# Order of epilogues, bank copies and weight preparation at the passage between two kinds of seven-product quads

## The chip, the cores and the metric

The kernel runs on one core of a Trainium2 chip. The core has a tensor engine (PE, with its own queue for weight loads), a vector engine (DVE), a scalar engine (ACT), GpSimd (POOL), and a sync engine (SP) that issues most transfers. Each engine works through its own instructions in order and waits on semaphores of the others. The metric is the device time of one launch in microseconds. Times are the median of three runs.

## The reference

Two blocks work on 512 tokens of 1024 features. The first block normalises and modulates its input (shift, scale and gate come from a small matrix product with a condition vector), runs a gated delta rule and a retention over chunks, projects, and ends with a gated feed-forward network. The second block has two layers, each of a feed-forward network, a mixer and another feed-forward network. So there are five feed-forward networks, all of this form:

```
def swiglu(h, w_in, w_out):
    gate, up = jnp.split(h @ w_in, 2, axis=-1)
    return (jax.nn.silu(gate) * up) @ w_out
x = x + g2 * swiglu(modulate(rms_norm(x, norm_ffn_g[layer]), sh2, sc2), w_ffn_in[layer], w_ffn_out[layer])
x = layer_norm(ALPHA * x + 0.5 * swiglu_2(x, ffn_w1[l, 0], ffn_w2[l, 0]), ln_g[l, 0], ln_b[l, 0])
```

All operands are float32. The hidden width of each network is 2816.

## The kernel before

**Precision.** A float32 matrix is held as two rounded parts, hi and lo. ACT casts hi, DVE subtracts to get lo (lines 79 to 81 for data, `cast` and `rest` at lines 163 to 166 for weights). A product is three matmuls: hi by hi, hi by lo, lo by hi.

**Seven products.** A product of 2 by 2 blocks is done with seven block products in place of eight (class `Quad`). Sums of weight blocks are made on DVE (`sum`, line 161). Sums of data blocks are made once, by `Left.sums` (lines 113 to 120), and split by `Left.puts`. The result blocks share partial results. A partial result is copied from one PSUM bank to another by ACT so that two products can go on from it: line 177 after product 1, lines 179, 180 and 181 after products 3, 4 and 5. The three banks that take copies are `sd0`, `sd1` and `sd2`. The other results lie in `pj` tiles.

**A feed-forward network** (`ffn`, line 285). Two units of hidden columns are done plainly with eight products, then the rest with quads, in four groups. Of a group, *gated quads* come first: they multiply the activations `XA` by the gate and up weights. When a result block is finished its *epilogue* runs: `c11` is a silu, `c12` (lines 257, 259) adds and multiplies and so gives half of a hidden tile `h`, `c12b` (line 260) splits that half into `hl`, `c22` subtracts, `c21` (lines 264, 265) gives the other half of `h`, `c21b` makes the sums of `h` and splits the second half, and `c21c` splits the sums. For the last gated quad of a group (`last`) all of `c21` is one step, `at_once`. Then come two *output quads* which multiply `hl` by the second weight matrix and add into `X`. They need the hidden tiles of all gated quads of the group. The first three groups end this way, the fourth in plain products. So each network has three places where the last gated quad of a group gives way to its output quads. They are called *passages* here: first, second and third passage of a network, fifteen in all. At the first and second passage an output quad has 3 hidden tiles (18 matmuls of 256 columns in a block product), at the third 2 (12 matmuls).

**What sets the order.** `run_quads` (line 190) writes the order of PE, ACT, DVE and SP out by hand. It goes step by step through the list of block products. At a step it issues the matmuls of product s, the epilogue and bank copy of product s-1 (`after`), the sums of weights, and the cast and lo part of the weights of product s+2. Normally the epilogue stands first and the weights after it. At a passage, after products 6 and 7 of the last gated quad, the flag `late` (line 224) puts weights first. At a passage the first products of both output quads follow each other, and only then come their other products (lines 197 to 201).

**The start of a network** (lines 308 to 317). While the plain units run, the sums of `XA` are made, part 1 of all four pairs of tiles and then part 0. They are called through `e.sums`. In the first network the modulated activations are not kept in `X`, so `sums` at line 1256 first adds hi and lo again (`again`, line 1253), two additions of 128x512 for a part of a pair.

**The condition product** (`ada_piece`, line 1261). Half rows of its weights are multiplied by the condition and added up over eight pieces. A ninth step sums over partitions by four matmuls. Parts 0 to 2 are done on ACT (scale, line 1276) and POOL (addition, line 1277), later parts on DVE (lines 1278, 1279). Parts 6 and 7 are issued in `first_b` during the projection that ends the first block's mixer.

Of the kernel before, what the change touches and what calls it, by code (L numbers as in the profile page):

```python
# [14 lines left out]
H0=slice(0,256); H1=slice(256,512); FULL=slice(0,512)  # L15
# [174 lines left out]
def run_quads(e, quads, extra):  # L190

    ET=mybir.EngineType
    seq=[]; left=None; done=set()
    for i,q in enumerate(quads):
        if q.needs and left: seq.append((left,7)); left=None
        if q not in done: seq.append((q,1))
        if q.needs: seq.append((quads[i+1],1)); done.add(quads[i+1])
        if left: seq.append((left,7))  # L200
        seq+=[(q,j) for j in (2,3,4,5,6)]; left=q
    seq.append((left,7))
    pos={(id(q),j):s for s,(q,j) in enumerate(seq)}
    at={}; free=-99
    for q in quads:
        g=lambda j: pos[id(q),j]
        for s,t in ((g(1)-6,0),(g(3)-9,5),(g(2)-8,6),(max(g(3)-6,free),3),(g(3)-4,1),(g(3)-3,2),(g(5),4)): at.setdefault(s,[]).append((q,t))
        free=g(5)-1
    with e.tc.manual_schedule(engines={ET.PE,ET.Activation,ET.DVE,ET.SP}):
        for s in range(min(at),len(seq)+1):  # L210
            for q,t in at.get(s,[]):
                if t in (0,5,6): q.load(e,t)
            put=None; keep=None
            if s>0: put=seq[s-1]
            if 0<=s<len(seq):
                q,j=seq[s]
                for d in q.needs:
                    if j==1: d.all(6)
                    if j==3: d.all(7)
                if j==2 and put==(q,1): q.after(e,1); put=None  # L220
                q.mm(e,j)
                if j==7 and s+1<len(seq) and seq[s+1][1]==2: keep=seq[s+1][0]
            nx=seq[s+2] if 0<=s+2<len(seq) else None
            late=put and put[1] in (6,7) and any(put[0] is q.needs[-1] for q in quads if q.needs)
            def weights():
                for q,t in at.get(s,[]):
                    if t in (1,2,3,4): q.sum(e,t)
                if nx and late: nx[0].cast(e,nx[1]); nx[0].rest(e,nx[1])
            if late: weights()
            if put and not (put[1]==1 and put[0] in done): put[0].after(e,put[1])  # L230
            if not late: weights()
            for q in quads:
                for j in (2,5,6,7):
                    if s>0 and (q,j)!=put: q.step(j)
            if keep in done: keep.after(e,1)
            for f in extra.get(s,[]): f()
            if nx and not late: nx[0].cast(e,nx[1]); nx[0].rest(e,nx[1])
        for q in quads:
            for j in (2,5,6,7): q.all(j)
# [11 lines left out]
def gated(e, H, i, hscale, sums, last):  # L251
# [11 lines left out]
    def c21(ps):  # L263
        g=tmp(e); nc.scalar.activation(g,ps,AF.Silu)
        nc.vector.scalar_tensor_tensor(u.h[:,2:4,:],pair(g),hscale,pair(u.t),op0=ALU.mult,op1=ALU.mult)
    v=nc.vector
    def part(p): u.s=H.sums(e,i,u.h[:,0:2,:],u.h[:,2:4,:],p,v,p and u.s); return u.s
    def c21b(ps):
        if sums: u.p0=part(0); u.p1=part(1)
        if last: H.puts(e,i,0,u.p0)  # L270
        H.second(e,i,u.h[:,2:4,:])
        if last: H.puts(e,i,1,u.p1)
    def c21c(ps):
        if sums and not last: H.puts(e,i,0,u.p0); H.puts(e,i,1,u.p1)
    u.c11,u.c12,u.c22,u.c21=[c11],[c12,c12b],[c22],[c21,c21b,c21c]
    if last:
        def at_once(ps): c21(ps); c21b(ps)
        u.c21=[at_once]
    return u

GAB=4
# [3 lines left out]
def ffn(e, w1, w2, acc, hscale, ln):  # L285

    nc=e.nc
    with ExitStack() as cf:
# [3 lines left out]
        H=Left(t,2,3); HP=Left(t,3,3)  # L292
# [17 lines left out]
                unit(j,sl)  # L310
                if j%2: into_left(e,H,j//2,hs[j//2],0 if sl is H0 else 1,False)
        for q in range(PLAIN-1): hsums(q)
        for p in (1,0):
            for i in range(4): e.sums(p,i)
        for j in range(halves,2*PLAIN):
            unit(j,FULL)
            for half in (0,1): into_left(e,H,j//2,hs[j//2],half,False)
# [1 line left out]
        for g,(j0,n) in enumerate(GROUPS):  # L319
            last=g==len(GROUPS)-1  # L320
# [86 lines left out]
class LN(Norm):  # L407
# [18 lines left out]
    def finish(s,sl):  # L426
        e=s.e; nc=e.nc; X=e.X; h=s.half[sl.start]
        ps=psum(e,"ps")
# [11 lines left out]
        for i in range(4):  # L440
# [4 lines left out]
                m=2*i+j; nc.scalar.activation(X[:,m,sl],d[:,j,:],AF.Identity,scale=s.g[:,m:m+1],bias=s.b[:,m:m+1])  # L445
                if s.out is not None: s.out(m,sl)
            if s.out is None: s.to_left(sl,i,X[:,2*i:2*i+2,sl])
        if sl is H1: e.sums=lambda part,i: e.XA.puts(e,i,part,e.XA.sums(e,i,X[:,2*i:2*i+2,H0],X[:,2*i:2*i+2,H1],part))

def proj_units(units, first):  # L450

# [781 lines left out]
class RMS(Norm):  # L1233
# [4 lines left out]
    def finish(s,sl):  # L1238
        e=s.e; nc=e.nc; X=e.X; h=s.half[sl.start]
        ps=psum(e,"ps"); tokstat2(e,ps,0,pair(h.Q),e.ones1024[:,0:1])  # L1240
# [12 lines left out]
        def again(i,o):  # L1253
            t=pair(tmp(e)); A=e.XA.t
            nc.vector.tensor_add(t,A[:,o:o+2,i,0,:].bitcast(F32),A[:,o:o+2,i,1,:].bitcast(F32)); return t
        def sums(part,i):
            a,b=[X[:,2*i:2*i+2,h] for h in (H0,H1)] if s.b is None else (again(i,0),again(i,2))
            e.XA.puts(e,i,part,e.XA.sums(e,i,a,b,part))
        if sl is H1: e.sums=sums

def ada_piece(e,D,at,part,k,tag,raw):

# [9 lines left out]
    raw=raw()  # L1272
    nc.sync.dma_start(raw,D["ada2"][16+part*4+k//2][:,(k%2)*512:(k%2)*512+512])
    c=e.cc[:,k,0:1]
    if part<3:
        nc.scalar.activation(acc if k==0 else raw,raw,AF.Copy,scale=c)
        if k: nc.gpsimd.tensor_add(acc,acc,raw)
    elif k==0: nc.vector.tensor_scalar(acc,raw,c,None,op0=ALU.mult)
    else: nc.vector.scalar_tensor_tensor(acc,raw,c,acc,op0=ALU.mult,op1=ALU.add)
# [109 lines left out]
```

## Time and profile before

| | |
|---|---|
| median of 3 runs | 3420.51 us (3419.1 to 3424.62) |
| profiled execution, whole | 3430.6 us |
| its span | 3428.8 us |
| PE busy | 3263.1 us (95%) |
| DVE busy | 2539.7 us (74%) |
| ACT busy | 1709.2 us (50%) |
| POOL busy | 199.3 us (6%) |
| TensorE clock granted, mean | 0.98 of full |

PE is busy almost throughout, so what matters are its few waits and the stretches in which its clock falls to half. A timeline row gives start, duration, engine, line, the operation and its operands. A bracket at its end tells how long the engine stood idle before it, and what it was waiting for. Matmul durations overlap a little, since matmuls are pipelined.

### The profile page before, as it was taken

The numbers are of one execution on the slowest core, as the hardware profiler recorded it, in microseconds if no ns is written. First come the engines' busy times: TensorE is split into PE (matmuls) and PEld (weight loads), VectorE is DVE, ScalarE is ACT, GpSimd is POOL, SyncE is SP. The second block draws the span as 40 slices with busy tenths as digits, with TensorE's granted clock in tenths as the row PEclk, the third lists the DMA queues.
The fourth block names the chain that finished last, engine by engine and source line by source line (L and its number), as shares of the span: only waits on it lengthen the run. The fifth ranks groups of instructions, "written<-read, shape, count | busy, mean of one in ns | idle before, by whom it ended". The sixth has DMA issues, their size and how long they took to land. (4 is left out here: it accounts for less than half of the span.)

```text
span 3428.8 us, 54643 instructions
## 1 busy us (share of the span) xinstructions
PE 3263.1 (95%) x22011; PEld 2989.2 (87%) x22011; DVE 2539.7 (74%) x4101; ACT 1709.2 (50%) x2640; POOL 199.3 (6%) x237
## 2 busy tenths in 40 slices
PE   6989889899999999999999999999999999999998
PEld 3767778899999999878889999999998788899998
DVE  5858877789968988653447888788976634368987
ACT  4544544455555555672224555545546822245554
POOL 3241221000000000110000000000000100000000
PEclk9999999999999999999999999999999999999999
DMA  6221214222332323333331233322332233322232
GB/s 207 67 70 44 74 57 141 82 97 96 100 114 74 105 99 99 99 93 97 95 116 52 91 102 104 102 71 93 99 107 97 94 97 99 98 83 85 93 105 62
DMA packets 103502, 322.09 MB, mean 94 GB/s; under 512 B 11472, under 2 KB 15184, under 8 KB 103248
## 3 DMA queue, kind: packets, MB, share of 16 engines
q1 hardware_dynamic: 102464, 316.04, 28.8%
q8 instruction: 173, 2.83, 0.3%
q0 software_dynamic: 640, 2.10, 0.2%
q14 instruction: 81, 0.66, 0.1%
q10 hardware_dynamic: 144, 0.45, 0.0%
HBM read 316.45 MB, written 2.10 MB: 93 GB/s over the span
## 5 line engine op out<-in xcount | busy, mean ns | idle before, releaser
L43 ACT CAST xa<-wraw 128x1024 fp32r<-128x1024 f32 (+1 forms) x200 | 202.4, 1016 | 385.2 <-PE pj L71 150.0
L166 DVE TENSOR_TENSOR wlo<-wraw,whi 128x1024 fp32r<-128x1024 f32 (+2 forms) x295 | 316.3, 1074 | 48.3 <-ACT whi L164 46.1
L70 PE MATMUL pj<-xa 128*128 128x512 f32 (+1 forms) x968 | 343.1, 355 | 1.4 <-ACT X L966 1.4
L72 PE MATMUL pj<-xa 128*128 128x512 f32 (+1 forms) x968 | 341.9, 354 | 0.0
L71 PE MATMUL pj<-xa 128*128 128x512 f32 (+1 forms) x968 | 341.3, 353 | 0.0
L44 DVE TENSOR_TENSOR xa<-wraw,xa 128x1024 fp32r<-128x1024 f32 (+1 forms) x190 | 224.5, 1184 | 110.0 <-ACT xa L43 108.1
L164 ACT CAST whi<-wraw 128x1024 fp32r<-128x1024 f32 (+2 forms) x295 | 272.3, 926 | 61.5 <-DVE wraw L161 26.2
L129 PE MATMUL sd<-xa,whi 128*128 128x256 f32 x1760 | 229.1, 283 | 0.0
L129 PEld LDWEIGHTS sd<-xa,whi 128*128 128x128 f32 x1760 | 219.1, 192 | 0.0
L129 PE MATMUL sd<-xa 128*128 128x256 f32 x1680 | 213.0, 283 | 0.0
L129 PEld LDWEIGHTS sd<-xa 128*128 128x128 f32 x1680 | 206.6, 192 | 0.0
L70 PEld LDWEIGHTS pj<-xa 128*128 128x128 f32 x968 | 187.1, 193 | 21.9 <-ACT X L966 1.8
L71 PE MATMUL sd<-xa 128*128 128x512 f32 (+1 forms) x600 | 204.7, 341 | 0.0
L70 PE MATMUL sd<-xa 128*128 128x512 f32 (+1 forms) x600 | 203.8, 341 | 0.9 <-DVE X L1230 0.9
L129 PE MATMUL pj<-xa,whi 128*128 128x256 f32 x1520 | 200.0, 285 | 4.2 <-ACT sd L177 4.2
L71 PEld LDWEIGHTS pj<-xa 128*128 128x128 f32 x968 | 187.2, 193 | 19.2
L72 PE MATMUL sd<-xa 128*128 128x512 f32 (+1 forms) x600 | 203.8, 340 | 0.0
L72 PEld LDWEIGHTS pj<-xa 128*128 128x128 f32 x968 | 186.9, 193 | 18.7
L129 PEld LDWEIGHTS pj<-xa,whi 128*128 128x128 f32 x1520 | 190.9, 193 | 5.9 <-ACT sd L177 5.5
L44 DVE TENSOR_TENSOR wlo<-wraw,whi 128x1024 fp32r<-128x1024 f32 (+1 forms) x88 | 109.1, 1241 | 97.6 <-ACT whi L43 97.1
L166 DVE TENSOR_TENSOR xa<-wraw,xa 128x1024 fp32r<-128x1024 f32 (+2 forms) x155 | 169.5, 1094 | 16.0 <-ACT xa L164 14.4
L43 ACT CAST whi<-wraw 128x1024 fp32r<-128x1024 f32 (+1 forms) x88 | 90.1, 1025 | 183.1 <-issue 93.2
(560 smaller groups left out, 8235.2 us busy)
## 6 DMA issues: line engine op xcount, KB each, us to landing
wraw<-in_f_dram SPq DMA_DIRECT2D x176, 512.0 KB, 4.0
wraw<-in_win_dram SPq DMA_DIRECT2D x144, 512.0 KB, 3.5
wraw<-in_f_dram SPq DMA_DIRECT2D x96, 384.0 KB, 3.2
wraw<-in_ff_dram SPq DMA_DIRECT2D x44, 512.0 KB, 4.0
raw<-in_ada_dram SPq DMA_DIRECT2D x48, 256.0 KB, 2.6
wraw<-in_ff_dram SPq DMA_DIRECT2D x24, 384.0 KB, 3.2
wraw<-in_ada_dram SPq DMA_DIRECT2D x16, 512.0 KB, 3.9
wraw<-in_f_dram SPq DMA_DIRECT2D x32, 256.0 KB, 2.8
```

Source lines behind the costliest of these rows:

```text
L43: nc.scalar.copy(hi[:,:n],raw[:,:n])
L44: (nc.gpsimd if e.wi%e.gp==0 else nc.vector).tensor_sub(lo[:,:n],raw[:,:n],hi[:,:n].bitcast(F32))
L70: nc.tensor.matmul(o,lhsT=hi[:,c],rhs=ah,start=start and k==k0,stop=False)
L71: nc.tensor.matmul(o,lhsT=hi[:,c],rhs=al,start=False,stop=False)
L72: nc.tensor.matmul(o,lhsT=lo[:,c],rhs=ah,start=False,stop=stop and k==nk-1)
L129: nc.tensor.matmul(ps[:,p*256:p*256+256],lhsT=w[:,j:j+128],rhs=A.t[:,c,k,l,:],start=first,stop=last,skip_group_check=True)
L164: s.w[j]=hilo_tile(e); e.nc.scalar.copy(s.w[j][0][:,:s.n],s.raw(j)[:,:s.n])
L166: hi,lo=s.w[j]; n=s.n; e.nc.vector.tensor_sub(lo[:,:n],s.raw(j)[:,:n],hi[:,:n].bitcast(F32))
```

## The change

There are four edits. First, at a passage only product 7 counts as `late`. After product 6 the epilogue `c12` now comes before the weights. Second, two new lines in `run_quads` finish what is left of the epilogue of product 6 (the split `c12b`) when the output quads' first product comes next, and finish the rest of `c21` of the last gated quad one step after the first product of an output quad. For this `c21` of the last gated quad is in two steps: `c21s` makes `h` and its sums, `c21p` splits them. Third, in the first network both parts of a pair's sums are made one after the other, from one pair of additions. Fourth, parts 6 and 7 of the condition product are scaled on ACT and added on POOL.

```
-            late=put and put[1] in (6,7) and any(put[0] is q.needs[-1] for q in quads if q.needs)
+            late=put and put[1]==7 and any(put[0] is q.needs[-1] for q in quads if q.needs)
...
             if not late: weights()
+            if s+1<len(seq) and seq[s+1][0].needs and seq[s+1][1]==1: put[0].all(6)
+            if s>1 and seq[s-1][0].needs and seq[s-1][1]==1: seq[s-1][0].needs[-1].all(7)
...
         if sums: u.p0=part(0); u.p1=part(1)
-        if last: H.puts(e,i,0,u.p0)
         H.second(e,i,u.h[:,2:4,:])
-        if last: H.puts(e,i,1,u.p1)
     def c21c(ps):
-        if sums and not last: H.puts(e,i,0,u.p0); H.puts(e,i,1,u.p1)
+        if sums: H.puts(e,i,0,u.p0); H.puts(e,i,1,u.p1)
...
-        def at_once(ps): c21(ps); c21b(ps)
-        u.c21=[at_once]
+        def c21s(ps): c21(ps); u.p0=part(0); u.p1=part(1)
+        def c21p(ps): H.puts(e,i,0,u.p0); H.second(e,i,u.h[:,2:4,:]); H.puts(e,i,1,u.p1)
+        u.c21=[c21s,c21p]
...
-        for p in (1,0):
-            for i in range(4): e.sums(p,i)
+        if e.again:
+            for i in range(4): e.sums((1,0),i)
+        else:
+            for p in (1,0):
+                for i in range(4): e.sums((p,),i)
...
-        def sums(part,i):
+        def sums(parts,i):
             a,b=[X[:,2*i:2*i+2,h] for h in (H0,H1)] if s.b is None else (again(i,0),again(i,2))
-            e.XA.puts(e,i,part,e.XA.sums(e,i,a,b,part))
-        if sl is H1: e.sums=sums
+            for p in parts: e.XA.puts(e,i,p,e.XA.sums(e,i,a,b,p))
+        if sl is H1: e.sums=sums; e.again=s.b is not None
...
-    if part<3:
+    if part<3 or part>5:
```

ACT at the first passage of the last network, before. `sd0` is the bank of product 7 of the last gated quad, `pj_29330` that of the first output quad's product 1, `hl` the split hidden tiles:

```order
L164 CAST whi_29287<-wraw_29120 128x768
L164 CAST xa_85<-wraw_29157 128x768
L80 CAST hl_28600<-h_29320 128x2x256
L164 CAST whi_29350<-wraw_29126 128x768
L264 ACTIVATE t_29354<-sd0_5189 128x512
L80 CAST hl_28600<-s_29357 128x2x256
L80 CAST hl_28600<-h_29320 128x256
L80 CAST hl_28600<-s_29360 128x2x256
L177 COPY sd1_5190<-pj_29330 128x512
L164 CAST whi_29389<-wraw_29120 128x768
```

The same place now:

```order
L164 CAST whi_29285<-wraw_29118 128x768
L80 CAST hl_28598<-h_29315 128x2x256
L164 CAST xa_85<-wraw_29155 128x768
L164 CAST whi_29348<-wraw_29124 128x768
L266 ACTIVATE t_29352<-sd0_5189 128x512
L177 COPY sd1_5190<-pj_29328 128x512
L80 CAST hl_28598<-s_29355 128x2x256
L80 CAST hl_28598<-h_29315 128x256
L80 CAST hl_28598<-s_29358 128x2x256
L164 CAST whi_29387<-wraw_29118 128x768
```

The bank copy has moved ahead of the three casts of the second half and its sums, and the cast of the first half ahead of one weight cast.

DVE at the same passage, before. Line 166 is the lo part of weights, 161 a sum of weights, 257 and 259 are `c12`, 81 is the lo part of `hl`, 265 is `c21`:

```order
L166 TENSOR_TENSOR wlo_29288<-wraw_29120,whi_29287 128x768
L161 TENSOR_TENSOR wraw_29122<-wraw_29122,wraw_29120 128x768
L166 TENSOR_TENSOR xa_85<-wraw_29157,xa_85 128x768
L257 TENSOR_TENSOR t_29318<-sd2_5191,t_29251 128x512
L259 SCALAR_TENSOR_TENSOR h_29320<-g0_29183,t_29318 128x512
L81 TENSOR_TENSOR hl_28600<-h_29320,hl_28600 128x2x256
L161 TENSOR_TENSOR wraw_29120<-wraw_29120,t3_29254 128x768
L166 TENSOR_TENSOR wlo_29351<-wraw_29126,whi_29350 128x768
L265 SCALAR_TENSOR_TENSOR h_29320<-t_29354,t_29285 128x512
```

And now (`c12` has lines 259 and 261, `c21` line 267):

```order
L166 TENSOR_TENSOR wlo_29286<-wraw_29118,whi_29285 128x768
L259 TENSOR_TENSOR t_29313<-sd2_5191,t_29249 128x512
L261 SCALAR_TENSOR_TENSOR h_29315<-g0_29181,t_29313 128x512
L161 TENSOR_TENSOR wraw_29120<-wraw_29120,wraw_29118 128x768
L81 TENSOR_TENSOR hl_28598<-h_29315,hl_28598 128x2x256
L166 TENSOR_TENSOR xa_85<-wraw_29155,xa_85 128x768
L161 TENSOR_TENSOR wraw_29118<-wraw_29118,t3_29252 128x768
L166 TENSOR_TENSOR wlo_29349<-wraw_29124,whi_29348 128x768
L267 SCALAR_TENSOR_TENSOR h_29315<-t_29352,t_29283 128x512
```

The pair `c12` has moved ahead of two weight operations, and a weight sum now stands between it and the lo part of `hl`.

DVE in the first network's start, now, for one pair of tiles. Line 1262 is the addition of hi and lo, lines 113 to 119 make the sums `s`, line 81 splits them:

```order
L1262 TENSOR_TENSOR t_6167<-xa_85 128x512
L81 TENSOR_TENSOR xa_85<-s_6154,xa_85 128x2x256
L81 TENSOR_TENSOR xa_85<-s_6160,xa_85 128x2x256
L116 TENSOR_TENSOR s_6169<-t_6165,t_6167 128x256
L118 TENSOR_TENSOR s_6169<-t_6165,t_6167 128x256
L113 TENSOR_TENSOR s_6175<-t_6167 128x256
L119 TENSOR_TENSOR s_6169<-s_6169 128x256
L114 TENSOR_TENSOR s_6175<-s_6175,t_6165 128x256
```

Both sums `s` of a pair now come from one pair of tiles `t`, so that there are eight additions of line 1262 in all where there were sixteen (line 1255).

## Rows read from the trace of the kernel before

**Rows 1.** The page, busy time of each engine.

```profile
PE 3263.1 (95%) x22011; PEld 2989.2 (87%) x22011; DVE 2539.7 (74%) x4101; ACT 1709.2 (50%) x2640; POOL 199.3 (6%) x237
```

**Rows 2.** Waits of PE: waiting line, releaser, us in total, times, longest.

```profile
PE pj L129 <- ACT sd L177: 33.1, 22, 2.2
...
PE pj L129 <- DVE wlo L166: 8.8, 5, 6.0
...
PE pj L129 <- DVE hl L81: 5.1, 15, 0.3
```

**Rows 3.** Timeline of PE, first passage of the last network.

```profile
3113.78 3.04 PE L129 MATMUL sd<-xa 128*128 128x256 f32 x24
...
3119.54 1.12 PE L129 MATMUL pj<-hl,whi 128*128 128x256 f32 x8
...
3122.83 2.32 PE L129 MATMUL pj<-hl,xa 128*128 128x256 f32 x18
3126.87 1.70 PE L129 MATMUL pj<-hl,whi 128*128 128x256 f32 x12 [1.72 <-ACT sd L177]
```

**Rows 4.** Timeline of ACT, same passage.

```profile
3124.89 0.62 ACT L80 CAST hl<-s 128x512 fp32r<-128x512 f32 x1 [2.79 <-DVE s L114]
...
3126.24 0.58 ACT L177 COPY sd<-pj 128x512 f32<-128x512 f32 x1
3126.75 0.82 ACT L164 CAST whi<-wraw 128x768 fp32r<-128x768 f32 x1
```

**Rows 5.** Timeline of DVE, same passage.

```profile
3117.07 0.95 DVE L161 TENSOR_TENSOR wraw<-wraw 128x768 f32<-128x768 f32 x1
...
3118.81 0.69 DVE L257 TENSOR_TENSOR t<-sd,t 128x512 f32<-128x512 f32 x1
...
3120.91 0.69 DVE L81 TENSOR_TENSOR hl<-h,hl 128x512 fp32r<-128x512 f32 x1 [0.69 <-ACT hl L80]
```

**Rows 6.** Timeline of PE, second passage of the last network.

```profile
3220.65 2.42 PE L129 MATMUL pj<-hl,xa 128*128 128x256 f32 x18 [1.72 <-ACT sd L177]
```

**Rows 7.** Timeline of PE, third passage of the last network and after.

```profile
3292.94 1.21 PE L129 MATMUL pj<-hl,whi 128*128 128x256 f32 x8 [2.15 <-ACT sd L177]
...
3317.43 1.22 PE L129 MATMUL pj<-xa,wlo 128*128 128x256 f32 x8 [0.57 <-DVE wlo L166]
```

**Rows 8.** Timeline of DVE, same stretch.

```profile
3287.51 0.69 DVE L81 TENSOR_TENSOR hl<-h,hl 128x512 fp32r<-128x512 f32 x1 [0.69 <-ACT hl L80]
...
3298.63 0.69 DVE L166 TENSOR_TENSOR wlo<-wraw,whi 128x512 fp32r<-128x512 f32 x1 [1.74 <-ACT whi L164]
```

**Rows 9.** Windows: stretch, length, PE, PEld, DVE, ACT, POOL, granted clock, DMA.

```profile
685.00:693.00 8.00, 6.74 (x30) 6.45 (x31) 6.01 (x7) 2.50 (x3) 0.00 (x0) 0.50 0.15 48
809.00:813.00 4.00, 4.00 (x21) 4.00 (x22) 2.17 (x4) 2.27 (x3) 0.00 (x0) 0.57 0.00 0
3294.00:3300.00 6.00, 6.00 (x40) 6.00 (x39) 4.11 (x8) 2.32 (x4) 0.00 (x0) 0.72 0.18 46
3300.00:3317.40 17.40, 16.86 (x140) 16.60 (x138) 17.22 (x25) 10.99 (x17) 0.00 (x0) 1.00 0.63 212
```

**Rows 10.** Timeline of PE, start of the first network.

```profile
679.04 0.49 PE L143 MATMUL sd<-xa,zero 128*128 128x512 f32 x1 [2.67 <-ACT t L300]
685.51 2.08 PE L129 MATMUL pj<-xa,wlo 128*128 128x256 f32 x8 [5.98 <-DVE wlo L166]
```

**Rows 11.** Timeline of DVE, same stretch: the additions of line 1255.

```profile
661.21 1.89 DVE L1255 TENSOR_TENSOR t<-xa 128x512 f32<-128x512 f32 x3
```

**Rows 12.** Additions of line 1277: engine, count, duration ns min/median/max, first and last start.

```profile
L1277 POOL TENSOR_TENSOR ada<-ada,raw x21: 1259/1284/2061, 73.2 to 264.3; 128x512 f32<-128x512 f32 x21
```

**Rows 13.** Timeline, an addition on POOL and one on DVE beside it.

```profile
207.28 1.27 POOL L1277 TENSOR_TENSOR ada<-ada,raw 128x512 f32<-128x512 f32 x1 [1.36 <-ACT raw L1276]
...
207.32 1.77 DVE L1153 TENSOR_TENSOR X<-X,t 128x512 f32<-128x512 f32 x1
```

**Rows 14.** Timeline of DVE: the end of part 6 of the condition product.

```profile
632.78 0.16 DVE L1270 TENSOR_TENSOR mod<-ps,vec 128x4 f32<-128x4 f32 x1
```

More of the change, by code (lines that the diff above doesn't have):

```diff
@@ L447, in finish @@
             if s.out is None: s.to_left(sl,i,X[:,2*i:2*i+2,sl])
-        if sl is H1: e.sums=lambda part,i: e.XA.puts(e,i,part,e.XA.sums(e,i,X[:,2*i:2*i+2,H0],X[:,2*i:2*i+2,H1],part))
+        if sl is H1:
+            def sums(parts,i):
+                for p in parts: e.XA.puts(e,i,p,e.XA.sums(e,i,X[:,2*i:2*i+2,H0],X[:,2*i:2*i+2,H1],p))
+            e.sums=sums; e.again=False
 def proj_units(units, first):
@@ L1255, in again, with sums @@
             nc.vector.tensor_add(t,A[:,o:o+2,i,0,:].bitcast(F32),A[:,o:o+2,i,1,:].bitcast(F32)); return t
-        def sums(part,i):
+        def sums(parts,i):
             a,b=[X[:,2*i:2*i+2,h] for h in (H0,H1)] if s.b is None else (again(i,0),again(i,2))
-            e.XA.puts(e,i,part,e.XA.sums(e,i,a,b,part))
-        if sl is H1: e.sums=sums
+            for p in parts: e.XA.puts(e,i,p,e.XA.sums(e,i,a,b,p))
+        if sl is H1: e.sums=sums; e.again=s.b is not None
 def ada_piece(e,D,at,part,k,tag,raw):
```

## The prediction

> **What bounds the kernel now.** I read the busy times first. PE is at work for 95% of the span, so time can only come from its waits and from stretches at half clock [rows 1]. In PE's waits the largest entry is the bank copy: matmuls that write a `pj` tile wait 33.1 us in 22 places for ACT's line 177 [rows 2]. Fifteen of those places are the passages. The 5.1 us in exactly 15 places for the lo part of `hl` belong to them too, 0.34 us each [rows 2]. A wait of 6.0 us for weights is the start of the first network [rows 2, 10].
>
> At the first passage of the last network, 24 matmuls take 3.04 us and 18 take 2.32 us, so one more matmul costs 0.12 us and a product of 18 costs 2.16 us [rows 3]. The first output quad's product 1 starts at 3119.54 and the second quad's at 3122.83. That is 3.29 us for 2.16 us of work, so 1.13 us are lost while `hl` is awaited. The second quad's product 1 should end at 3124.99, but the next one starts at 3126.87, 1.88 us later, because the bank copy is not there. The bracket says 1.72 us; I count start to start. So a passage costs 3.0 us.
>
> Why the copy is late stands in ACT's rows. Its source is complete by about 3122.9, but it starts at 3126.24, behind three casts of which the first waited 2.79 us for DVE's sums [rows 4]. `hl` is late because DVE does a weight sum from 3117.07 and a lo part before it begins `c12` at 3118.81, although product 6, which `c12` needs, is over at 3113.78 + 3.04 = 3116.82 [rows 3, 5].
>
> Some pauses cost a second time. After the pause at the second passage of the first network the granted clock is 0.57 over 4 us (full speed is 2.4 GHz, the lower level 1.2), which is 4 x 0.43 = 1.7 us of lost work. At the third passage of the last network it is 0.72 over 6 us, again 1.7 us [rows 9]. Three second and three third passages show such a fall in this execution; the others do not, with pauses as long: 1.72 us at the last network's second passage [rows 6].
>
> **The change part by part.** *The first product of the output quads.* `c12` moves ahead of two weight operations and can start at 3117.07 instead of 3118.81, 1.74 us earlier. The weight sum that now stands between it and the lo part of `hl` takes 0.87 us start to start and fills the 0.69 us in which DVE idled there [rows 5]. So the lo part starts some 1.5 us earlier, more than the 1.13 us that PE lost. That loss goes.
>
> *The bank copy.* It no longer stands behind casts that wait for DVE. It needs the first quad's product 1, which would now end at 3119.54 + 2.16 = 3121.70, and takes 0.58 us [rows 4]. The second quad's product 1 then runs until 3123.86, so the copy is hidden with 1.5 us to spare. The 1.88 us go.
>
> *What is late next.* The third product needs its weights cast, and ACT does that behind the casts of `hl`, which follow DVE. DVE's queue comes earlier only by the idle time that goes, 0.69 us [rows 5]. The first of the casts then starts at 3124.89 - 0.69 = 3124.20. From there to the start of the weight cast were 1.86 us, less 0.52 us for the copy which stood between; the cast takes 0.82 us [rows 4]. It is done at 3126.36. PE wants it at 3119.54 + 3 x 2.16 = 3126.02. So 0.34 us of the wait come back, and the first passage gains 3.0 - 0.34 = 2.7 us. The weights moved behind the epilogue (the second product's lo part and the sums) are used two products later and have over 1 us to spare. Bounds: 0.7 us (only DVE's shift counts) to 3.0 us.
>
> *Second passages* have the same wait [rows 6] and tile sizes, and the same moves: 2.7 us. Five first and five second passages: **27 us** (7 to 30).
>
> *Third passages* have products of 12 matmuls and a wait of 2.15 us for the copy [rows 7], but from there on DVE is the limit: it is busy for 17.22 of the 17.40 us before the next wait, and PE then stands for its weights [rows 7 to 9]. DVE does the same work as before, so all that is gained is the idle time it loses: 0.69 us at `hl` [rows 8] and some 0.3 us of small gaps. **5 us** for five (3.5 to 12). Where the clock falls, DVE also idles for 1.74 us [rows 8].
>
> *Start of the first network.* PE waits 2.67 and then 5.98 us there [rows 10], and DVE works without a pause until the weights that end the wait. Eight of sixteen additions go. Three take 1.89 us with the last one's 0.69 us in it, so one costs 0.60 us: **4.8 us** (4.8 to 5.6).
>
> *Condition product.* Fourteen additions of 1.28 us on POOL [rows 12] are 18 us, starting at about 592 us and done by some 612 us. Its result is used at 632.78 [rows 14], so POOL's slowness is hidden, and so is what DVE no longer does, since PE waits in that stage for almost nothing. What speaks against it: while an addition ran on POOL from 207.28 to 208.55, an addition on DVE of the same shape took 1.77 us [rows 13], where one alone takes 0.69 us [rows 11]. An addition of the norm's statistics can so be held up to 1.3 us, with PE behind it: **-0.6 us** (0 to -1.3). The Trainium skill, "SBUF — State Buffer", section "SBUF: two separate sides", says that a VectorE operation with two SBUF inputs and a GpSimd one that reads SBUF exclude each other for a whole instruction; the row agrees, 1.77 = 0.69 + about 1.1. By it alone every such pair would be dearer, 14 x 1.28 = 18 us of DVE time at most, and DVE frees more than half of that in the stage.
>
> *Clock.* The pauses that brought the falls go, so three second passages give 3 x 1.7 = **5.1 us** and three third ones, bounded by DVE's 1.74 us, 3 x 1.4 = **4.2 us**. At the start a pause of about 4 us is left, so I leave its slow clock (0.50 over 8 us [rows 9]) as it is.
>
> *Sum.* Against the profiled execution of 3430.6 us: 27 + 5 + 4.8 - 0.6 = 36.2 us of pauses, and 9.3 us of clock, 45.5 us in all, gives 3385. The timed median is 10.1 us below the profiled execution. I do not know whether timed runs have as many clock falls. With none of them the gain is 36.2 us (3384.3), with all 45.5 us (3375.0). I take a point between: **3381 us**. The Trainium skill, "TensorE: Matmul & The Clock Gate", section "Part 1: The HAM clock gate", says that the activity window runs freely and so differs from run to run; equal pauses with and without a fall here agree, and by it any share of the 9.3 us may be in a timed run.
>
> **The rivals.** *The third product takes the wait.* If ACT and DVE come no earlier than by DVE's 0.69 us and have no slack, each of the ten first and second passages gains 0.7 us and the clock still falls: 7 + 3.5 + 4.8 = 15 us, 3405. For it: DVE is 74% busy and the chain from `c21` to the casts stays. Against it: the cast of the third product's weights ended at 3127.57 [rows 4], well before PE's third product at 3129.03.
>
> *Nothing comes back.* All passages lose their whole 3.0 us (30 us), third ones keep 2 us each (10 us), and the clock stays up at the start too: about 52 us, 3368. Against it: DVE is full after the third passages.
>
> *Slower: DVE waits for product 6.* `c12` now stands in front of weights, and DVE works in order. If product 6 is not over when `c12` comes to the head, DVE idles with a weight sum, two lo parts and `c21` queued behind, and the wait moves into weights. At the first passage product 6 is over 0.25 us before [rows 3, 5]. Were it a whole product of 24 later (2.88 us), `c12` would start 0.9 us later than now, each passage would cost 0.9 us more, and with clock falls at more of them (1.7 us) 15 x 0.9 + 6 x 1.7 - 4.8 = 19 us, 3439. It decides from 1.7 us of lateness on; the rows show none.
>
> *Hardly anything.* The gains end in waits a few products later, because weights are just in time all over: within 7 us of 3420. Against it: PE shows no waits of that kind between passages.
>
> **How the numbers follow.** Forecast 0.63, third product 0.13, nothing back 0.16, hardly anything 0.04, slower 0.04. The range takes in the forecast with both shares of the clock and "nothing comes back", and goes up to where the third product keeps most of its wait: 3368 to 3403. A measurement of this kernel can tell about 0.2%, 6.8 us, from no change. Faster 0.92, same 0.04, slower 0.04.
>
> **What would show it.** In the profile after, PE's waits for ACT's line 177 should fall from 33.1 us to about 5 us (the seven that are no passages), and those for the lo part of `hl` at passages to none. A small wait, 0.3 us, should stand before the third product of the first output quad, for weights. After third passages the wait for weights should be longer than the 0.57 us of before. At the start of the first network PE should be about 5 us earlier behind the same kind of wait. The windows behind second passages should show full clock. The prediction is wrong if new waits of 2 us stand at the passages for `hl` sums or weights, if DVE shows idle time before `c12`, or if PE waits for the condition product.

## The result and the profile after

The changed kernel takes 3385.2 us (median of 4 runs, 3381.45 to 3387.36), the kernel before beside it 3422.57 (4 runs). The ratio is 0.9886, with a 95% interval of 0.9875 to 0.9898. The profiled execution took 3385.55 us, 45.05 us less than the profiled one of before. In a second set of four runs the changed kernel took 3381.3 us (ratio 0.9873, 0.9851 to 0.9895), 42.3 us less than the kernel before (3423.59, all its runs up to then).

The page, busy time of each engine, answers to [rows 1]:

```profile
PE 3247.4 (96%) x22011; PEld 2976.4 (88%) x22011; DVE 2531.2 (75%) x4077; ACT 1715.4 (51%) x2656; POOL 219.9 (6%) x251
```

The waits of PE, with the columns of [rows 2]:

```profile
PE sd L129 <- ACT whi L164: 7.3, 15, 1.0
...
PE pj L129 <- DVE wlo L166: 6.6, 5, 3.7
PE pj L129 <- ACT sd L177: 5.1, 7, 1.0
```

The copy wait is down from 33.1 us in 22 places to 5.1 in 7, and the waits for `hl` at the passages are gone. A smaller new wait stands in their place at all fifteen: the third product's cast weights.

First passage of the last network on PE, against [rows 3], and then ACT, against [rows 4]:

```profile
3083.67 1.60 PE L129 MATMUL pj<-hl,whi 128*128 128x256 f32 x12
...
3085.83 2.32 PE L129 MATMUL pj<-hl,xa 128*128 128x256 f32 x18
3087.99 1.60 PE L129 MATMUL pj<-hl,whi 128*128 128x256 f32 x12
...
3090.53 1.70 PE L129 MATMUL sd<-hl,whi 128*128 128x256 f32 x12 [0.21 <-ACT whi L164]
```

```profile
3086.03 0.57 ACT L177 COPY sd<-pj 128x512 f32<-128x512 f32 x1 [0.79 <-PE pj L129]
3088.29 0.62 ACT L80 CAST hl<-s 128x512 fp32r<-128x512 f32 x1 [1.69 <-DVE s L114]
...
3089.65 0.83 ACT L164 CAST whi<-wraw 128x768 fp32r<-128x768 f32 x1
```

The two first products take 2.16 us each without a break. The copy now waits for its source (0.79 us) and is over at 3086.60, well before PE wants its bank at 3087.99. The third product should start at 3083.67 + 3 x 2.16 = 3090.15. It starts at 3090.53, so 0.38 us come back. From the first to the third product are 6.86 us, where before they were 3129.12 - 3119.54 = 9.58: 2.72 us less. The third product before:

```profile
3129.12 1.60 PE L129 MATMUL sd<-hl,whi 128*128 128x256 f32 x12
```

DVE at the same place, against [rows 5]:

```profile
3081.21 0.68 DVE L259 TENSOR_TENSOR t<-sd,t 128x512 f32<-128x512 f32 x1
...
3082.54 0.95 DVE L161 TENSOR_TENSOR wraw<-wraw 128x768 f32<-128x768 f32 x1
3083.41 0.68 DVE L81 TENSOR_TENSOR hl<-h,hl 128x512 fp32r<-128x512 f32 x1
```

The weight sum stands between `c12` and the lo part, with no idle time before the lo part.

Third passage of the last network and the wait after it, PE, against [rows 7]:

```profile
3251.35 1.21 PE L129 MATMUL sd<-hl,whi 128*128 128x256 f32 x8 [1.02 <-ACT whi L164]
...
3273.45 1.22 PE L129 MATMUL pj<-xa,wlo 128*128 128x256 f32 x8 [0.58 <-DVE wlo L166]
```

Start of the first network, PE, against [rows 10]:

```profile
675.43 0.62 PE L143 MATMUL sd<-xa,zero 128*128 128x512 f32 x2
...
682.28 2.08 PE L129 MATMUL pj<-xa,wlo 128*128 128x256 f32 x8 [3.73 <-DVE wlo L166]
```

Windows of after, with the columns of [rows 9]: the start of the first network, behind that network's second passage, and behind the last network's third passage.

```profile
680.00:688.00 8.00, 4.97 (x21) 4.67 (x22) 7.70 (x10) 2.52 (x4) 0.00 (x0) 0.63 0.00 0
797.00:801.00 4.00, 4.00 (x35) 4.00 (x34) 3.91 (x8) 1.52 (x4) 0.00 (x0) 1.00 0.00 0
3252.00:3258.00 6.00, 6.00 (x51) 5.96 (x51) 5.82 (x11) 3.69 (x7) 0.00 (x0) 1.00 0.45 129
```

The clock stays up behind the passages, where before it was 0.57 and 0.72.

Where the 45.05 us came from, by the starts of the first products at the passages in both traces:

| stretch | us less |
|---|---|
| five first passages (2.38 in the first network, 2.61 to 2.65 in the others) | 12.9 |
| five second passages (2.63 and 2.64 in two, 3.67 to 4.87 in the three with a slow clock before) | 17.9 |
| five third passages (1.58, 2.98, 3.60, 0.73 with a mixer in the stretch, 2.84) | 11.7 |
| up to the first passage of the first network | 3.7 |
| second network's end to the third's first passage | -2.3 |
| end of the program | 1.1 |

### The profile page after: what moved, and what is told of

It reads as the page before. It is cut to its first block, busy times and chain, and to the rows that moved or that the text cites. A ratio compares the mean times of both kernels' runs of the same rounds, so it can differ in the third digit from the quotient of the medians.

```text
span 3383.7 us, 54654 instructions
## 1 busy us (share of the span) xinstructions
PE 3247.4 (96%) x22011; PEld 2976.4 (88%) x22011; DVE 2531.2 (75%) x4077; ACT 1715.4 (51%) x2656; POOL 219.9 (6%) x251
## 4 chain that ended last, share of the span: by engine, by line
PE 73%; DVE 15%; ACT 6%; issue 4%; POOL 1%; DMA 1%; SPq 0%; ACTq 0%; DVEq 0%; POOLq 0%
PE sd L129 17%; PE pj L129 13%; PE pj L70 7%; PE pj L71 6%; PE pj L72 6%; PE sd L71 5%; PE sd L70 5%; PE sd L72 5%; DVE wraw L161 2%; DVE wlo L166 1%; DVE cv L929 1%; PE ps L371 1%; DVE xa L44 1%; DMA wraw<-in_f_dram 1%; DVE hl L81 1%
```

## The experiments

A "stretch" is the time between two such starts. Of each kind the shortest of the five networks is given, so that no slow clock is in it.

**The passages' two edits alone**, on the kernel before (the new `late`, the two `all` lines, `c21` in two steps; no change to `e.sums` and `ada_piece`).

> The kernel before with the two edits at the passages alone (epilogue of product 6 ahead of weights, bank copy ahead of the casts of the second half). Theory of the prediction: the fifteen passages give 32 us in pauses and up to 9 us in clock, so 33 to 40 us under the kernel before and within 6 us of the changed kernel. In the profile PE's waits for the bank copy fall to 7 places and about 5 us, and the third product of the first output quad waits 0.2 us at first and second passages and 1.0 us at third ones for a weight cast. Rival, that the start of the first network carries a good part: less than 25 us.

Measured: 3382.5 us, ratio 0.9883 (0.9865 to 0.9901), 40.9 us below the kernel before (3423.38 in this set). The passages carry the whole gain; the other two edits, one a gain and one a loss, are told apart below. Its first-to-second stretch is 91.18 us and its second-to-third 70.99, as in the changed kernel.

**Only `c12` ahead of the weights.**

```
-            late=put and put[1] in (6,7) and any(...)
+            late=put and put[1]==7 and any(...)
```

> Only the flag: the epilogue of product 6 ahead of the weights, the bank copy still behind the casts of the second half. Theory: the vector queue comes 0.69 us earlier, the casts and the copy behind them come 0.69 us earlier, and PE cannot go on before the copy. So 15 x 0.7 = 10 us, PE's wait for hl at the first product goes, and its wait for the copy grows from 1.72 to about 2.1 us, in 22 places still. Rival, that the two waits of a passage are independent: 15 x 1.13 = 17 us, with the wait for the copy unchanged.

Measured: 3409.38 us, ratio 0.9961 (0.9949 to 0.9973). PE at the last network's first passage in this kernel:

```profile
3098.70 1.96 PE L129 MATMUL pj<-hl,whi 128*128 128x256 f32 x12
...
3101.22 2.32 PE L129 MATMUL pj<-hl,xa 128*128 128x256 f32 x18
3105.26 1.70 PE L129 MATMUL pj<-hl,whi 128*128 128x256 f32 x12 [1.72 <-ACT sd L177]
```

The second quad's first product comes 2.52 us after the first one (3101.22 - 3098.70) instead of 3.29. A product takes 2.16, so 0.36 us of the 1.13 are still lost there: without the second edit the split into `hl` still stands behind a weight operation. The copy's wait is as long as ever, and not 2.1 us. A first passage gains 0.78 us and a third one 0.60 (table below), 10.8 us in fifteen places: the size that the theory gives (0.69 each), not the 1.13 of its rival. The rest of the 14.0 us in the whole time is not in these pauses.

**Only the rest of `c21` behind the copy** (the `all` lines and `c21s`, `c21p`; `late` as before).

> Only the second edit: the bank copy ahead of the casts of the second half, the epilogue of product 6 still behind the weights. Theory: PE's wait for the copy goes at all fifteen passages, its waits for hl at the first product stay (0.34 us in 15 places). First and second passages gain 1.9 us each, third ones about 0.3 us since the vector engine loses little idle time: 20 us, and up to 9 us more where clock falls go. Rival, that the third product takes the wait: 7 us or less.

Measured: 3393.6 us, ratio 0.9918 (0.9900 to 0.9937). PE, same passage:

```profile
3092.05 1.12 PE L129 MATMUL pj<-hl,whi 128*128 128x256 f32 x8
3093.43 0.38 PE L129 MATMUL pj<-hl,whi 128*128 128x256 f32 x1 [0.27 <-ACT hl L80]
3094.16 0.61 PE L129 MATMUL pj<-hl,whi 128*128 128x256 f32 x3 [0.34 <-DVE hl L81]
...
3095.32 2.32 PE L129 MATMUL pj<-hl,xa 128*128 128x256 f32 x18
3097.48 1.60 PE L129 MATMUL pj<-hl,whi 128*128 128x256 f32 x12
```

Here the waits for `hl` stay and the copy's goes. It was expected to give 20 us in pauses and gives 23.7: 1.91 us at first and second passages, as expected, and 0.92 at third ones, where 0.3 was expected. The stretches of the four kernels side by side:

| us | before | only `c12` | only copy | both |
|---|---|---|---|---|
| first to second passage | 93.82 | 93.04 | 91.91 | 91.18 |
| second to third passage | 73.62 | 72.84 | 71.71 | 70.99 |
| second network's third passage to its last products | 93.25 | 92.65 | 92.33 | 91.75 |

(93.25 is from the kernel with only the first network's edit, whose passages are those of before, since the profiled execution of before had a slow clock there.) At first and second passages the two gains add up: 0.78 + 1.91 = 2.69 by themselves, 2.64 together. That they do so this closely is partly luck: alone, the first edit leaves 0.36 us of its wait, and together the third product takes back 0.38. The rival by which the third product takes the wait is out, since by it a passage gains 0.7 us. At third passages they give 0.60 + 0.92 = 1.52, together 1.50.

**Parts 6 and 7 of the modulation left on DVE**, else the changed kernel.

```
-    if part<3 or part>5:
+    if part<3:
```

> The changed kernel with parts 6 and 7 of the condition product back on the vector engine. Theory after the profile: the sixteen pieces on ACT and POOL cost about 1.3 us, because POOL's additions hold up the vector engine's additions of the norm's statistics. So 1 to 2 us faster than the changed kernel, less than a timing tells, and in the profile PE's waits for lnQ at about 610 us are 0.6 us in one place instead of 1.6 in two. Rival, that taking the pieces off the vector engine gave something: 0 to 3 us slower.

Measured: 3375.67 us, ratio 0.9866 (0.9848 to 0.9883), 9.5 us below the changed kernel's first median, where 1 to 2 were expected. Both traces, row against row, differ by 3.1 us at 58 to 64 us from the start, long before the edit. The window 58:64, first of the changed kernel, then of this one:

```profile
58.00:64.00 6.00, 5.80 (x11) 1.17 (x11) 1.92 (x5) 1.09 (x2) 0.00 (x0) 0.50 0.37 136
```

```profile
58.00:64.00 6.00, 6.00 (x27) 3.15 (x27) 2.99 (x6) 4.12 (x6) 0.00 (x0) 1.00 0.88 306
```

More of the kind stood at 578, 1360 and 1457 us. So the same two kernels were run again, in a new set of runs.

> The changed kernel once more, beside the same kernel with the scaling of the modulation left on DVE. In the first profiles those two were 11 us apart, of which 1.2 to 1.6 us stood where the edit acts (two products that wait for lnQ around 606 us, DVE held by POOL's additions) and 7 to 8 us at four places that the edit does not touch, each with a lower granted clock in the slower one (3.1 us at 58 to 64 us, 0.8 at 578, 1.8 at 1360, 1.0 at 1457). Theory: these clock falls change from one loading of a program to the next and are no part of the edit; then the two medians now lie 1 to 4 us apart. Rival: the falls belong to the program; then they lie 8 to 11 us apart again, and the falls stand at the same four places.

> The changed kernel with the scaling and the additions of modulation parts 6 and 7 left on DVE, once more. Theory (the clock falls come with the loading): 1 to 4 us below the changed kernel beside it. Rival (they belong to the program): 8 to 11 us below it, with 64 us to 61 us for the first product after the timestep network again.

Measured: 3381.3 us for the changed kernel and 3379.41 for the other (3376.62 to 3382.33), 1.9 us apart with runs that overlap. The slow clock at 58 to 64 us now stands in both. Most of the 9.5 us was not the edit's: it changes from one set of runs to the next. (That it comes with the loading, as the theory has it, is more than the runs show: each set has one trace, and the two runs of the kernel with DVE were on different chips, so loading, chip and chance are not told apart.)

What is left is local. From the zeroing at the last norm (about 555 us) to the first passage the changed kernel takes 149.19 us both times, the one with DVE 146.19 and 145.77. But not all of these 3.0 to 3.4 us is the edit's. At about 577 us, ahead of the norm's products, both traces of the changed kernel have the lower clock for longer. These are the same 35 matmuls (the rows count some at the edges too) in the changed kernel, and in a kernel of a later experiment that does the same work up to 877 us:

```profile
570.63:582.13 11.50, 9.31 (x38) 7.84 (x38) 9.06 (x33) 5.43 (x8) 1.08 (x2) 0.70 0.49 151
```

```profile
571.46:581.53 10.07, 7.88 (x38) 6.81 (x37) 7.77 (x31) 5.43 (x8) 1.07 (x2) 0.83 0.43 140
```

The edit does not decide which it is: in the fourteen traces of all kernels these matmuls take 10.0 to 10.1 us eight times and 11.5 us six times, and either comes with the edit and without it. Like with like, the stretch in us:

| slow clock at about 577 us | parts 6 and 7 on ACT and POOL | on DVE |
|---|---|---|
| longer | 149.19, 149.19, 149.22 | 146.67 |
| shorter | 151.96 | 146.19, 145.77 |

(149.22 and 151.96 are from the kernels with added multiplications below, 146.67 from the last experiment; what they change comes later.) So the edit costs 2.5 us where PE comes 1.4 us later anyhow, and 5.8 to 6.2 where it does not. Two products of the norm wait for the statistics, first in the changed kernel, then in the one of 151.96 us:

```profile
609.85 0.38 PE L371 MATMUL ps<-ones,lnQ 128*128 128x1 f32 x2 [0.61 <-DVE lnQ L403]
611.26 0.83 PE L371 MATMUL ps<-ones,lnQ 128*128 128x1 f32 x6 [1.03 <-DVE lnQ L403]
```

```profile
610.58 0.38 PE L375 MATMUL ps<-ones,lnQ 128*128 128x1 f32 x2 [1.94 <-DVE lnQ L407]
611.98 1.44 PE L375 MATMUL ps<-ones,lnQ 128*128 128x1 f32 x6 [1.02 <-DVE lnQ L407]
```

Behind the second pair the granted clock is 0.50 from 612 to 615 us, behind the first it stays at 1.00.

**Scaled on ACT, added on DVE.** This tells POOL's additions from ACT's scalings.

```
-        if k: nc.gpsimd.tensor_add(acc,acc,raw)
+        if k: (nc.gpsimd if part<3 else nc.vector).tensor_add(acc,acc,raw)
```

> Parts 6 and 7 of the modulation scaled on ACT as in the changed kernel, but added on DVE instead of POOL. Theory: what the edit costs is POOL's additions of two SBUF operands holding DVE's; then no DVE operation of 128x8 takes over 0.3 us between 585 and 620 us (1.14 in the changed kernel) and no lnQ addition over 0.5 us (1.47), and the first two products of the norm wait 0 and 0.8 us for lnQ instead of 0.61 and 1.03. Rival: the cost is ACT's 18 scalings in the way of its other work; then these waits stay, and ACT is named as the releaser of DVE there. In the whole time 1 to 2 us at the most, which the clock may cover.

(ACT's instructions in the two profile pages, 2640 before and 2656 now, make it 16 scalings and not 18.)

Measured: 3381.73 us, ratio 0.9876 (0.9858 to 0.9894). All additions of line 403, duration in ns min/median/max, of the changed kernel and then of this one:

```profile
L403 DVE TENSOR_TENSOR lnQ<-lnQ,t x96: 412/418/1528, 594.8 to 3369.0; 128x256 f32<-128x256 f32 x96
```

```profile
L403 DVE TENSOR_TENSOR lnQ<-lnQ,t x96: 413/420/426, 594.4 to 3366.3; 128x256 f32<-128x256 f32 x96
```

Without POOL none of the 96 is slow, so it is POOL that holds them. But the second wait did not become 0.8 us:

```profile
611.48 0.83 PE L371 MATMUL ps<-ones,lnQ 128*128 128x1 f32 x6 [1.63 <-DVE lnQ L403]
```

DVE now stands in its own queue, with the additions and a chain of 128x8 operations ahead. The stretch from the zeroing is 149.00 us, with the shorter slow clock at 577 us (10.05 us for the 35 matmuls), so it stands between 151.96 with POOL and 146.19 and 145.77 without the edit. POOL's hold on DVE is shown, and moving only the additions gives back 3.0 us, about half, as far as one trace each can tell. What the other 2.8 to 3.2 us are, DVE's queue or ACT's scalings (the rival), is not told apart. ACT has a part in the changed kernel too: one of its squares for the statistics (line 402) starts at 606.46 us behind four scalings, 0.52 us after its input is done.

**Only the modulation's edit**, on the kernel before.

> The kernel before with only parts 6 and 7 of the modulation scaled on ACT and added on POOL. Theory: POOL's additions hold DVE's of two SBUF operands; so the norm's products around 609 us wait for lnQ twice (0.6 and 1.0 us) as in the changed kernel, and the stretch from the last norm to the first passage grows by 1.5 to 3.5 us over the 151.8 of before; the time 1 to 4 us over the kernel before, which its clock may cover. Rival: these waits came only with the other edits; then the stretch stays within 0.5 us.

Measured: 3425.37 us against 3424.93 for the kernel before, ratio 1.0002 (0.9992 to 1.0011). The norm's products wait 1.79 and 1.02 us for the statistics, where before one of them waited 0.64, and behind these waits the clock is at half:

```profile
609.00:612.00 3.00, 3.00 (x15) 3.00 (x15) 2.99 (x3) 1.96 (x3) 2.88 (x2) 0.50 0.53 176
```

The stretch from the zeroing is 156.21 us, 4.4 more than the 151.78 of before (both with the shorter slow clock at 577 us) and beyond the 3.5 expected, by what the half clock costs. The whole time can't tell it from nothing.

**Only the first network's additions**, on the kernel before.

> The kernel before with only the first network's additions made once for both sums. From the last norm (zeroing at about 556 us) to the first passage the kernel before takes 151.8 us and the one with the passages' edits alone 152.4. Theory: 8 additions of 0.60 us go from DVE while PE waits for the low weights, so this stretch becomes 147 us (4.8 less), the first wait for low weights 3.7 us instead of about 6, and nothing after it changes; the time about 3419. Rival: PE waits for the copies into banks there and not for DVE's additions; then the stretch stays above 150 us.

Measured: 3420.39 us, ratio 0.9986 (0.9975 to 0.9996). The stretch from the zeroing is 146.10 us, 5.7 less than before, and the wait for weights is 3.74 us:

```profile
676.87 2.08 PE L129 MATMUL pj<-xa,wlo 128*128 128x256 f32 x8 [3.74 <-DVE wlo L166]
```

The other pair of kernels that differs by this edit alone, the passages' edits without and with it, gives 152.37 - 146.19 = 6.2 us. Of this 0.5 us stand ahead of the additions: the first of the two has the longer slow clock at 577 us, 1.4 us, and then waits 0.9 us less for the statistics. So both pairs give 5.7 us, and PE did wait for DVE's additions.

**Is DVE the limit behind third passages?** Three more multiplications of 128x384 on DVE at the first output quad behind each third passage, and in another kernel behind each first passage.

```
+        if extra:
+            for _ in range(3): e.nc.vector.tensor_mul(e.dm,e.dm,e.dm)
         into(m,H0,ps,1,True)
```

> The changed kernel with three more multiplications of 128x384 on DVE (about 0.47 us each, 1.4 us together, same result) in the stretch after each network's third passage, five times in all. Theory: DVE is what is late there (19.19 of 19.40 us busy), so each lengthens the stretch by about 1.4 us, the wait of 0.58 us for low weights at its end grows by as much, and the whole time by about 7 us (0.2%). Rival: PE or ACT is late there as in the other passages, and DVE has room; then no wait grows and the time stays within 1 us.

> The same three multiplications at the same place after each network's first passage instead. Theory: there DVE has room once the passage is over, so they cost 0 to 1 us in all, no stretch from a first to a second passage grows by over 0.3 us (91.2 us in the changed kernel), and the time is that of the changed kernel. Rival: DVE is late there too; then each costs 1.4 us and the stretch becomes 92.6 us.

Measured: 3390.16 us behind third passages and 3383.46 behind first ones (3385.2 and 3381.3 without). A multiplication took 0.557 us, so three are 1.67. Behind third passages the three stretches that can be compared grew by 1.71, 1.68 and 1.64 us, all that was added. The wait for low weights, though, stayed at 0.57. The added time shows earlier:

```profile
1233.66 0.74 PE L129 MATMUL sd<-hl,wlo 128*128 128x256 f32 x4 [0.27 <-DVE wlo L166]
...
1236.78 1.71 PE L129 MATMUL sd<-hl,xa 128*128 128x256 f32 x12 [0.95 <-ACT sd L181]
```

Behind first passages each stretch grew too, by 0.47 us in two networks and by 1.1, 1.3 and 1.8 in the others, 5.1 us together, where 1 at the most was expected. This is the second network's on PE, and then on ACT:

```profile
1070.54 2.41 PE L129 MATMUL sd<-hl,xa 128*128 128x256 f32 x18 [0.23 <-ACT sd L181]
1073.52 1.70 PE L129 MATMUL pj<-hl,whi 128*128 128x256 f32 x12 [0.57 <-ACT sd L177]
```

```profile
1072.15 0.83 ACT L164 CAST whi<-wraw 128x768 fp32r<-128x768 f32 x1 [1.66 <-DMA wraw<-in_f_dram]
1072.89 0.58 ACT L177 COPY sd<-pj 128x512 f32<-128x512 f32 x1
```

ACT stands 1.66 us for a transfer of weights, with the copy that PE wants queued behind. Without the multiplications ACT stands there too (1.74 us), but this cast starts at 1072.77 in a network that runs 2.19 us later in the trace, so relative to PE it has come 1.57 us later, nearly all that was added to DVE. The likely way is the weight buffer: in both traces the transfer is issued 0.06 us after one of DVE's weight sums (line 161) ends, at 1069.67 without the multiplications and 1069.14 with them. That was not tried by itself. ACT waits for such a transfer in the second and the fifth network; the first network's 1.1 us has none in it. So DVE is the limit behind third passages, and behind first ones its room of 1.2 us (1.67 - 0.47) is gone where such a transfer comes next. The theory that it has plenty there is wrong.

**The weight cast ahead of the casts of the second halves**, with the modulation on DVE: `c21p` cut in two, its second part behind the cast. `held` is the last gated quad, at the step in question.

```
+            if held: held.step(7)
...
             if nx and not late: nx[0].cast(e,nx[1]); nx[0].rest(e,nx[1])
+            if held: held.all(7)
...
-        def c21p(ps): H.puts(e,i,0,u.p0); H.second(e,i,u.h[:,2:4,:]); H.puts(e,i,1,u.p1)
-        u.c21=[c21s,c21p]
+        def c21p(ps): H.puts(e,i,0,u.p0)
+        def c21q(ps): H.second(e,i,u.h[:,2:4,:]); H.puts(e,i,1,u.p1)
+        u.c21=[c21s,c21p,c21q]
```

> Modulation left on DVE, and at every passage the weight cast for the third product ahead of the two copies into banks of the second halves. Theory: the third product's wait for its weights (0.2 us at each of 10 first and second passages and more where passages follow the start of the network, 1.0 at 5 third ones, 7.0 us in 15 places) goes at the first and second passages and stays at the third, where DVE is what is late; so this wait falls to about 5 us in 5 places and the time is 2 to 3 us below the kernel with modulation on DVE. Rival: the casts of the second halves are then late for the fourth product, a new wait of 0.3 to 0.6 us at each passage, and the time is equal or up to 5 us more.

Measured: 3375.95 us (3372.51 to 3381.1), ratio 0.9861 (0.9841 to 0.9882). Waits of PE:

```profile
PE pj L129 <- ACT sd L177: 6.6, 10, 1.0
...
PE sd L129 <- ACT sd L181: 3.5, 5, 0.8
PE sd L129 <- ACT whi L164: 1.0, 5, 0.2
```

The third product's wait fell from 7.0 to 1.0 us, also at third passages, where it was expected to stay. There the same time is waited for a copy a little later (line 181, 3.5 us in 5 places), which fits DVE being what is late there. Three new copy waits of line 177 (10 places instead of 7) take back 1.3 us (6.6 against 5.3 in the kernel with the cast behind): the rival is right in part. From first to third passage the five networks take 2.1 us less in all than with the cast behind. In whole times it is 3.5 us below that kernel and 5.3 below the changed one of the same set, each time with runs that overlap. So it is well below the kernel before, but not shown to be better than the changed kernel with its modulation on DVE.

## Why the prediction was right, point by point

The forecast was 3381 us, and the medians were 3385.2 and 3381.3. At the passages the mechanism was the one that happened; the condition product is the term that was mis-sized. Term by term:

*First and second passages*, 2.7 us each. Measured 2.72 from the first to the third product, and 2.61 to 2.65 in the stretches with full clock (2.38 in the first network, whose third product waits 0.27 us longer). The copy gives 1.91 alone, against 1.88. Of the 1.13 for `hl` the first edit alone gives 0.78, the rest goes only with both. The third product's wait, forecast at 0.34, is 0.38. Counting a passage from start to start and asking for the next late thing was the right way.

*Third passages*, 1.0 us each. Measured 1.5: the term was too small by 0.5 each, 2.5 us in all. The reason given was right, since DVE behind them gives no time away and an added 1.67 us costs 1.67. What was undercounted is DVE's idle time. By windows from the passage to the wait for weights, it went from 1.66 us to 0.30 in a network with full clock, and the stretch from 29.11 to 27.59 us. The rows are the kernel with only the first network's edit, and then the changed one:

```profile
1224.43:1253.54 29.11, 26.06 (x211) 25.18 (x209) 27.45 (x43) 17.83 (x30) 0.00 (x0) 1.00 0.40 137
```

```profile
1218.98:1246.57 27.59, 25.89 (x210) 25.12 (x209) 27.29 (x44) 17.22 (x29) 0.00 (x0) 1.00 0.42 144
```

The prediction also said that the wait for weights behind the passage would be longer than 0.57 us. It is 0.58. PE came no earlier to that product, since the new wait of 1.02 us at the third product holds it back before.

*Start of the first network*, 4.8 us. The additions did what was worked out: the pauses of 2.67 and 5.98 us became none and 3.73, 4.9 less. The stretch gained 5.7. The rest, which I had left out, is the clock: after the wait it is at 0.50 and comes back sooner. Before, PE goes on at 685.51 and the granted clock is 0.68 from 692 to 694 us; now it goes on at 682.28 and the clock is 0.77 from 688 to 690 us. That the shorter pause is the cause was not tried by itself.

*Condition product*, -0.6 us (0 to -1.3). This term was mis-sized. The waits for the statistics grew by 1.0 us (1.64 against 0.64) in the changed kernel and by 2.2 in the kernel with this edit alone. Like with like the stretch lost 2.5 us and 5.8 to 6.2 in the changed kernel and 4.4 in the kernel with this edit alone, the larger figures with a clock that falls behind the waits. I had priced one held addition of the statistics (1.3 us); in the chain that ends in these waits two are held in the changed kernel, 1.42 us at 604.13 and 1.47 at 606.89. And I had said that DVE's shorter work there is hidden, but not that its small operations stand in the way too. DVE and POOL, first in the changed kernel:

```profile
591.97 8.30 POOL L1284 TENSOR_TENSOR ada<-ada,wraw 128x512 f32<-128x512 f32 x6 [11.90 <-PE sd L72]
592.06 0.48 DVE L1297 SCALAR_TENSOR_TENSOR X<-sd,mod,X 128x256 f32<-128x256 f32 x1
...
593.56 1.14 DVE L593 TENSOR_TENSOR p<-p,z 128x8 f32<-128x8 f32 x1
```

and then in the kernel without POOL there:

```profile
595.31 0.16 DVE L593 TENSOR_TENSOR p<-p,z 128x8 f32<-128x8 f32 x1
```

An operation of 128x8 takes 1.14 us beside an addition on POOL and 0.16 without one. It ends with POOL's running instruction, however small it is itself: the second of the six additions runs from 593.37 to 594.68 us, and the slow operation ends at 594.70. The operation of line 1297, which reads a PSUM tile, keeps its 0.48 us, and one of line 594 with a single SBUF operand takes 0.17 us at 593.36, beside the same addition. The rule of the Trainium skill weighed in the prediction ("SBUF — State Buffer", "SBUF: two separate sides") says so for two SBUF inputs, and the trace agrees.

*Clock*, 9.3 us in the profiled execution. The three second passages with a slow clock gained 1.0 to 2.2 us beyond the 2.64 of the others, 4.8 in all against 5.1 (in the first of them the changed kernel has 0.46 us of small waits later in the stretch). The three third ones gained 1.5, 2.1 and 1.3 beyond 1.5 us, against 4.2 us in all; the middle one has other work in its stretch, so the last us of it is not sure.

*Sum.* The profiled execution became 45.05 us shorter, the forecast being 45.5 to 3385, and the median 37 (42 in the second set). That nearness is in part luck: third passages and the start gave 3.4 us more than forecast, the condition product, with the slow clock ahead of it at 577 us, 2.4 to 2.8 less, and slow clocks at 1360 and 1457 us, which the second set's trace does not have, took 3.9 us in the profiled execution.

## What to carry to other kernels

Where several engines hand work round, find for each wait of the bound engine what stands in front of the awaited instruction in its own queue; if that is work which waits for a third engine, moving the one behind the other can give its whole wait, as the bank copy did. Two such waits in one chain do not simply add up: each edit alone is bounded by what is late next (0.78 of 1.13 us here), and the next late thing has to be priced. Moving additions from a busy engine to an idle one is no gift if both read SBUF: look for small two-input operations of the busy engine in that stage. And a difference of some microseconds between two kernels should be read from stretches of the trace, since here one kernel's median moved by 4 us from one set of runs to the next. Even then compare traces that have the same slow clock ahead of the place: the cost of the condition product is 2.5 or about 6 us according to it.

## What the runs showed of the hardware that was not expected

Medians of the same kernel in two sets of runs differ: 3385.2 and 3381.3 us, 3375.67 and 3379.41. In the traces much of the difference lies in short stretches at the lower clock behind pauses of PE, as at 58 to 64 us, where the clock granted was 0.50, 1.00, 0.72 and 0.57 in the four profiled executions of two kernels that are alike up to there. At about 577 us the same 35 matmuls take either 10.0 to 10.1 or 11.5 us in fourteen traces, and nothing in between. What decides which pause is followed by a slow clock stays open.

A small DVE operation of two SBUF operands beside an addition on POOL takes seven times its own time (1.14 us against 0.16), and a later transfer of weights can reach PE through an ACT copy that only stands behind its cast.
